# Token mixers of a hybrid decoder trunk: state products, scores and key transposes grouped over two or four token tiles

## The chip, the cores and the metric

One Trainium2 chip, one of its cores. The engines named here: PE (TensorE, matrix multiplies; PEld is its weight load), DVE (VectorE), ACT (ScalarE), POOL (GpSimd), SP (SyncE, which issues all DMAs of this kernel, in order). The metric is the device time of one execution in microseconds (us), the median of several runs; lower is better.

## The reference, cut to what matters

A two-layer decoder trunk works on a prompt of 2048 tokens of width 1024, and on eight single decode tokens. In a layer, the normalized input is multiplied by one wide projection, and its columns feed four token mixers, each a quarter of the width: A, RetNet retention; H, HGRN2; S, an S5 state space; M, Mamba-2 SSD. Their gated outputs are joined, projected by `w_out` and added to the residual. A, H and M are the same chunked recurrence, with four heads of 64 in each:

```
o_inter = einsum('bchk,bhkv->bchv', qc * exp(cum), h)          # queries against the carried state
scores  = einsum('bthk,bshk->bhts', qc, kc) * decay             # inside the chunk, causal
h_new   = exp(total) * h + einsum('bshk,bshv->bhkv', k_end, vc) # state product
o       = o_inter + einsum('bhts,bshv->bthv', scores, vc)
```

The state `h` goes from chunk to chunk. Head norm, gate and the projection follow.

## The kernel before, in words

The prompt is cut into four blocks of 512 tokens (TB), in each of two layers: eight blocks. A block is four token tiles of 128 (`tt` from 0 to 3). A Python program writes out all instructions; a list scheduler then orders each engine's instructions when the program is built, by the order in which they were written (with some offsets) and by when their inputs and buffers are expected, and adds all waits. At run time every engine works off its own list in that order.

`ORDER` is the order of writing for one block: `A`, `H`, `M`, `S` are its projections, `a`, `h`, `s`, `m` its mixers, `O` the output projection, `n`/`N` the norm for the next block, and a `^` means the block before. So a mixer is written next to projections that do not depend on it, and the scheduler places their matmuls (L647 in `gemm_wide`, L590 and L622 in `gemm`) between the mixer's steps. Weights come by DMA into raw slabs (`wr`, NWR = 7 buffers), ACT rounds them (L606, L642) and DVE makes the rest (L607, L643) into `wh` (NWH = 6 buffers); three matmuls in fp32r make one product. The first block of each layer also carries the decode tokens, for which PE multiplies with the raw slab itself (L595, L652).

PSUM has eight banks: five (`gb`) for projections, three (`mb`, `mbank()`) for all else, mixers included. Work tiles come from pools: `half` (10 buffers of 512 values per partition), `big` (9 of 1024).

Matmuls of the mixers are in float32, which the trace records as two passes for each matmul (transposes as one). `halves()` gives r = 0, 1: partitions 0 to 63 and 64 to 127. A matmul whose operands have only 64 rows (scores, L1093), or whose result has only 64 partitions (outputs L1108, L1227, L1462; state products L1113, L1233, L1468), uses half of the array.

`mix_A`, for each of the four tiles: four transposes into one bank (L1085), a copy to `qf` (L1087), scores into two banks, one for each r (L1093), multiplied by the decay mask (L1096), queries against the state `hA` (L1102), scores against values (L1108), the state product into its own bank `sp` (L1113), four DVE updates of the state into the other of two buffers (L1119). After each second tile `head_post` norms and gates the output bank `ob`, and at the end `mix_store` transposes the result (L663). `mix_H` first builds its scores in seven levels (L1183 to L1206); then, for each tile, queries against the state (L1221), scores against values (L1227), the state product (L1233) and the update (L1240), with key transposes for two tiles at a time (L1215). `mix_M`, for each tile: transposes (L1437, L1438), a decay matrix by POOL, PE and ACT (L1445 to L1449), scores (L1451) and their mask (L1453), outputs (L1462), queries against the state (L1465), the state product (L1468), the update (L1471, L1472) and the gated output.

Of the kernel before, what the change touches and what calls it, by code (L numbers as in the profile page):

```python
# [44 lines left out]
NWR = 7  # L45
# [7 lines left out]
NHN = 8  # L53
NACT = 2
# [62 lines left out]
def trunk_kernel(ctx: ExitStack, tc: tile.TileContext, A: dict):  # L117
# [959 lines left out]
    def mix_A(L, B):  # L1077
        nonlocal hA
        ogs = []
        ob = None  # L1080
        for tt in range(4):
            qk = lambda i: B.qk(tt, i)
            ps = mbank()
            for i in range(4):
                T.transpose(ps[:, i * P : (i + 1) * P], qk(i), ident)  # L1085
            qf = half()
            S.copy(qf, ps)  # L1087
            sm = half()
            smv = sm.rearrange("p (a r t) -> p a r t", a=2, r=2)
# [8 lines left out]
            if tt % 2 == 0:  # L1098
                ob = mbank()
            for p in range(2):  # L1100
                oc = (tt % 2) * 256 + p * P
                T.matmul(ob[:, oc : oc + P], qf[:, p * P : (p + 1) * P], hA[:, p, :], start=(tt % 2 == 0 and p == 0), stop=False)  # L1102
            for p in range(2):
                oc = (tt % 2) * 256 + p * P
                for r in range(2):
                    h = 2 * p + r
                    for u in range(2):
                        T.matmul(ob[64 * u : 64 * u + 64, oc + r * 64 : oc + (r + 1) * 64], sm[:, h * P + 64 * u : h * P + 64 * u + 64],  # L1108
                                 B.rv[:, tt, h * 64 : (h + 1) * 64], start=False, stop=(tt % 2 == 1 and h == 3))
            sp = mbank()  # L1110
            for p in range(2):
                for r, sl in halves():
                    T.matmul(sp[sl, p * 64 : (p + 1) * 64], qk(2 + p)[:, sl], B.rv[:, tt, p * P + 64 * r : p * P + 64 * r + 64],  # L1113
                             start=True, stop=True)
            zi[2] += 1
            hn_ = hAs[zi[2] % 2]
            for p in range(2):
                for r, sl in halves():
                    V.scalar_tensor_tensor(hn_[sl, p, sl], hA[sl, p, sl], mats[sl, M_GS + p : M_GS + p + 1],  # L1119
                                           sp[sl, p * 64 : (p + 1) * 64], ALU.mult, ALU.add)  # L1120
            hA = hn_
            if tt % 2 == 1:
                og = half([P, 4, 2, 64])
                head_post(ob.rearrange("p (t a v) -> p t a v", t=4, a=2),
                          B.rg[:, tt - 1 : tt + 1, :].rearrange("p x (b a v) -> p (x b) a v", b=2, a=2), og)
                ogs.append(og.rearrange("p t a v -> p (t a v)"))
        mix_store(B.mix, 0, lambda tt: ogs[tt // 2][:, (tt % 2) * 256 : (tt % 2) * 256 + 256], L.ret_w)
# [25 lines left out]
    def mix_H(L, B):  # L1153
# [54 lines left out]
        ogs = []  # L1208
        for tt in range(4):
            t2 = tt % 2  # L1210
            if t2 == 0:
                kps = mbank()
                for j in range(2):
                    for p in range(2):
                        T.transpose(kps[:, j * 256 + p * P : j * 256 + (p + 1) * P], k[:, p, (tt + j) * P : (tt + j + 1) * P], ident)  # L1215
                kT = half()
                S.copy(kT, kps)
                ob = mbank()
            for p in range(2):
                oc = t2 * 256 + p * P  # L1220
                T.matmul(ob[:, oc : oc + P], q[:, p, tt * P : (tt + 1) * P], hH[:, p, :], start=(t2 == 0 and p == 0), stop=False)  # L1221
            for p in range(2):
                oc = t2 * 256 + p * P
                for r in range(2):
                    h = 2 * p + r
                    for u in range(2):
                        T.matmul(ob[64 * u : 64 * u + 64, oc + r * 64 : oc + (r + 1) * 64], st[p][:, tt * 2 + r, 64 * u : 64 * u + 64],  # L1227
                                 B.gi[:, tt, h * 64 : (h + 1) * 64], start=False, stop=(t2 == 1 and h == 3))
            sp = mbank()
            for p in range(2):  # L1230
                for r, sl in halves():
                    c = p * P + 64 * r
                    T.matmul(sp[sl, p * 64 : (p + 1) * 64], kT[:, t2 * 256 + c : t2 * 256 + c + 64], B.gi[:, tt, c : c + 64],  # L1233
                             start=True, stop=True)
            zi[1] += 1
            hn_ = hHs[zi[1] % 2]
            for p in range(2):
                for r, sl in halves():
                    c = slice(64 * r, 64 * r + 64)
                    V.scalar_tensor_tensor(hn_[sl, p, c], hH[sl, p, c], tot[sl, p, tt : tt + 1],  # L1240
                                           sp[sl, p * 64 : (p + 1) * 64], ALU.mult, ALU.add)
            hH = hn_
            if t2 == 1:
                og = half([P, 4, 2, 64])
                head_post(ob.rearrange("p (t a v) -> p t a v", t=4, a=2),
                          B.gg[:, tt - 1 : tt + 1, :].rearrange("p x (b a v) -> p (x b) a v", b=2, a=2), og)
                ogs.append(og.rearrange("p t a v -> p (t a v)"))
# [160 lines left out]
    def mix_M(L, B):  # L1408
# [23 lines left out]
        ogs = []  # L1432
        for tt in range(4):
            tsl = slice(tt * P, (tt + 1) * P)
            tps = mbank()
            for j in range(2):
                T.transpose(tps[:, j * P : (j + 1) * P], xm[:, j, tsl], ident)  # L1437
            T.transpose(tps[:, 256:384], Bm[:, tsl], ident)  # L1438
            xb = half([P, 384])
            S.copy(xb, tps[:, 0:384])  # L1440
            xmT = xb[:, 0:256].rearrange("p (h v) -> p h v", h=4)
# [8 lines left out]
            cb = mbank()  # L1450
            T.matmul(cb[:, 0:256], Bm[:, tsl], cz[:, :, tsl], start=True, stop=True)  # L1451
# [3 lines left out]
            V.tensor_tensor(lv, lv, cbm[:, :, None, :].to_broadcast([P, 2, 2, P]), ALU.mult)  # L1455
            vv = half([P, 2, 4, 64])
            V.tensor_tensor(vv[:, 0], xmT, dt[:, tt, :][:, :, None].to_broadcast([P, 4, 64]), ALU.mult)
            V.tensor_tensor(vv[:, 1], vv[:, 0], ec[:, 1, tt, :][:, :, None].to_broadcast([P, 4, 64]), ALU.mult)
            ob = mbank()
            for h in range(4):  # L1460
                for u in range(2):
                    T.matmul(ob[64 * u : 64 * u + 64, h * 64 : (h + 1) * 64], lm[:, h * P + 64 * u : h * P + 64 * u + 64],  # L1462
                             vv[:, 0, h, :], start=True, stop=True)
            for g in range(2):
                T.matmul(ob[:, 256 + g * P : 256 + (g + 1) * P], cz[:, g, tsl], hM.rearrange("p a v -> p (a v)"), start=True, stop=True)  # L1465
            sp = mbank()
            for g in range(2):
                T.matmul(sp[64 * g : 64 * g + 64, 0:P], xb[:, 256 + 64 * g : 256 + 64 * g + 64],  # L1468
                         vv[:, 1, 2 * g : 2 * g + 2, :].rearrange("p a v -> p (a v)"), start=True, stop=True)
            hn_ = small([P, 2, 64], "hM")  # L1470
            V.tensor_tensor(hn_, hM, et[:, tt, :][:, :, None].to_broadcast([P, 2, 64]), ALU.mult)  # L1471
            V.tensor_tensor(hn_, hn_, sp[:, 0:P].rearrange("p (a v) -> p a v", a=2), ALU.add)  # L1472
            hM = hn_
# [18 lines left out]
            ogs.append(og)  # L1492
        mix_store(B.mix, 6, lambda tt: ogs[tt], L.m2_w)
# [145 lines left out]
    def phase(ph, i):  # L1639
# [6 lines left out]
        elif ph == "a":  # L1646
            if first:
                hA = zeroed(hAs[zi[2] % 2])
# [10 lines left out]
        elif ph == "h":  # L1659
            if first:  # L1660
                zi[1] += 1
                hH = zeroed(hHs[zi[1] % 2])
# [26 lines left out]
        elif ph == "m":  # L1689
            if first:  # L1690
                hM = zeroed(small([P, 2, 64], "hM"))
# [85 lines left out]
```

## Time and profile before

| | us |
|---|---|
| median of three runs | 2353.92 |
| runs, from lowest to highest | 2349.15 to 2357.65 |
| span of the profiled execution, from its first to its last instruction | 2351.3 |
| its PE busy | 2186.8 (93%) |
| its DVE busy | 1690.8 (72%) |
| its ACT busy | 1007.4 (43%) |

The profiled execution's own time is given as its span alone; the median is of separate executions. "Busy" of PE is the union of its modelled matmul times; a matmul's record is longer than the distance to the next one, since they are pipelined, so the pace is read from start times. A line such as L1093 is that of the kernel's file; L663 and the other lines of helpers collect the work of several callers. In the timeline each row is a run of like instructions: its start, its length, the engine, the line and the tiles, how many; in brackets the idle time before it and what ended that.

### The profile page before, as it was taken

To read this page: it belongs to the slowest core of one execution; us is meant where nothing else is said; L and a number is where in the kernel's file an instruction comes from. 1 tells how busy PE (TensorE), PEld (TensorE's weight loads), DVE (VectorE), ACT (ScalarE), POOL (GpSimd) and SP (SyncE) were. 2 spreads that over 40 slices of the span, in tenths; PEclk is the share of its full clock that TensorE was granted. 3 is DMA by queue.
4 is the path that set the end of the run, shared out by engine and by line. 5 is a ranking of instruction groups with operands and counts; after the bars stand their busy time and mean duration, and the time that the engine had idled before them with its cause. 6 is when DMAs were issued, how large, how long until landed. Compare 5 with 4: busy or idle time off the path is not lost.

```text
span 2351.3 us, 41033 instructions
## 1 busy us (share of the span) xinstructions
PE 2186.8 (93%) x15047; PEld 1724.8 (73%) x15047; DVE 1690.8 (72%) x4625; ACT 1007.4 (43%) x1873; POOL 247.0 (11%) x212
## 2 busy tenths in 40 slices
PE   7997899999989999999899987999999999999897
PEld 6766676686767877788676775776877787777687
DVE  6778885578866687558856588855985568766686
ACT  5334545245442353424534245443454344443543
POOL 1020011001111011001110001100011001100100
PEclk9998899999999999999999998999999999999998
DMA  5334543433434644251333424526244352337222
GB/s 190 89 95 103 159 154 76 129 107 118 133 101 147 139 126 141 75 167 47 125 126 114 134 65 153 162 46 182 86 153 157 104 175 64 95 122 260 64 65 83
DMA packets 259226, 283.89 MB, mean 121 GB/s; under 512 B 88208, under 2 KB 184608, under 8 KB 259024
## 3 DMA queue, kind: packets, MB, share of 16 engines
q1 hardware_dynamic: 259024, 281.26, 39.8%
q8 instruction: 119, 1.95, 0.3%
q14 instruction: 83, 0.68, 0.1%
HBM read 245.00 MB, written 31.99 MB: 118 GB/s over the span
## 4 chain that ended last, share of the span: by engine, by line
PE 57%; DVE 20%; issue 6%; ACT 3%; DMA 2%; SPq 1%; POOL 1%; ACTq 0%; DVEq 0%; POOLq 0%
PE gb L647 25%; PE gb L622 10%; PE gb L590 5%; DVE big L1191 2%; PE mb L1332 1%; PE mb L1183 1%; DVE wh L643 1%; PE mb L569 1%; DMA big<-s5c 1%; DVE hHb L1240 1%; DVE half L1299 1%; PE gb L652 1%; PE mb L663 1%; SPq L940 1%; PE mb L1198 1%
## 5 line engine op out<-in xcount | busy, mean ns | idle before, releaser
L647 PE MATMUL gb<-wh,hn 128*128 128x512 f32 x2208 | 558.0, 402 | 4.9 <-DVE wh L643 4.3
L622 PE MATMUL gb<-hn,wh 128*128 128x512 f32 x1920 | 491.5, 403 | 0.1
L647 PEld LDWEIGHTS gb<-wh,hn 128*128 128x128 f32 x2208 | 408.1, 190 | 110.3 <-issue 13.5
L622 PEld LDWEIGHTS gb<-hn,wh 128*128 128x128 f32 x1920 | 348.9, 188 | 89.4 <-issue 8.8
L642 ACT CAST wh<-wr 128x512 fp32r<-128x512 f32 x296 | 182.7, 620 | 375.9 <-PE gb L647 184.5
L647 PE MATMUL gb<-wh,mx 128*128 128x512 f32 x1344 | 338.0, 402 | 0.0
L643 DVE TENSOR_TENSOR wh<-wr,wh 128x512 fp32r<-128x512 f32 x296 | 208.6, 712 | 170.5 <-ACT wh L642 169.6
L607 DVE TENSOR_TENSOR wh<-wr,wh 128x512 fp32r<-128x512 f32 (+1 forms) x248 | 176.9, 724 | 169.5 <-ACT wh L606 163.6
L647 PEld LDWEIGHTS gb<-wh,mx 128*128 128x128 f32 x1344 | 247.7, 189 | 63.5 <-issue 6.9
L606 ACT CAST wh<-wr 128x512 fp32r<-128x512 f32 (+1 forms) x248 | 151.6, 621 | 268.1 <-PE gb L647 103.8
L590 PE MATMUL gb<-wh,hn 128*128 128x256 f32 (+1 forms) x1728 | 233.3, 291 | 4.2 <-DVE hn L553 4.1
L590 PEld LDWEIGHTS gb<-wh,hn 128*128 128x128 f32 x1728 | 218.2, 194 | 13.3 <-DVE hn L553 5.9
L1445 POOL TENSOR_TENSOR half<-mats,m_lal 128x512 fp32r<-128x512 f32 x64 | 71.7, 1148 | 511.1 <-DVE m_lal L1423 301.6
L1183 PE MATMUL mb<-zb,big 128*64 128x64 f32 x1536 | 66.5, 242 | 38.8 <-ACT zb L1176 31.5
L1191 DVE COPY_PREDICATED big<-lvl,mb 64x256 f32<-64x256 int32 x192 | 93.0, 537 | 10.3 <-PE mb L1183 6.4
L1176 ACT COPY zb<-big 64x512 f32<-64x512 f32 x112 | 70.3, 628 | 64.0 <-DVE big L1204 54.2
L1183 PEld LDWEIGHTS mb<-zb,big 128*64 128x64 f32 x1536 | 56.6, 152 | 53.5 <-ACT zb L1176 38.2
L1166 POOL TENSOR_TENSOR big<-mats,h_dg 128x1024 f32<-128x1024 f32 x16 | 34.0, 2140 | 557.8 <-DVE h_dg L1163 438.5
L1367 DVE SCALAR_TENSOR_TENSOR big<-gb,vt,big 128x511 f32<-128x511 f32 (+2 forms) x96 | 66.9, 739 | 12.0 <-ACT big L1365 11.8
L671 ACT ACTIVATE half<-mb 128x512 f32<-128x512 f32 x32 | 19.1, 598 | 88.3 <-PE mb L1227 47.8
L1348 DVE TENSOR_TENSOR half<-half,big 128x512 f32<-128x512 f32 x16 | 10.9, 687 | 63.1 <-ACT half L1347 63.1
L1042 POOL TENSOR_TENSOR half<-half,half 128x256 f32<-128x256 f32 x32 | 27.2, 850 | 235.0 <-DVE half L1040 85.2
(493 smaller groups left out, 3240.7 us busy)
## 6 DMA issues: line engine op xcount, KB each, us to landing
wr<-in_w_in SPq DMA_DIRECT2D x416, 256.0 KB
wr<-in_w_out SPq DMA_DIRECT2D x128, 256.0 KB
big<-s5c SPq DMA_DIRECT2D x56, 512.0 KB
xn<-xmid SPq DMA_DIRECT2D x32, 512.0 KB
xn<-in_x_prompt SPq DMA_DIRECT2D x24, 512.0 KB
xmid<-half SPq DMA_DIRECT2D x44, 256.0 KB
half<-xmid SPq DMA_DIRECT2D x44, 256.0 KB
half<-in_x_prompt SPq DMA_DIRECT2D x32, 256.0 KB
```

What stands on the lines that cost most here:

```text
L590: T.matmul(out, lhs[2 * ks[ki] + k][:, a, tt * P : (tt + 1) * P], hls[ki][:, c, k, :n], start=(ki == 0 and k == 0 and pi == 0 and tt % per ...
L606: S.copy(hl[:, 0, :, :n], raw[:, :, :n])
L607: V.tensor_tensor(hl[:, 1, :, :n], raw[:, :, :n], hl[:, 0, :, :n].bitcast(F32), ALU.subtract)
L622: T.matmul(banks[i], hl[:, a, k, i * P : (i + 1) * P], lhs[2 * k2 + k][:, c, :], start=(ki == 0 and k == 0 and pi == 0), stop=(ki == 3 and ...
L642: S.copy(hl[:, 0, 0:512], raw[:, 0:512])
L643: V.tensor_tensor(hl[:, 1, 0:512], raw[:, 0:512], hl[:, 0, 0:512].bitcast(F32), ALU.subtract)
L647: T.matmul(banks[tt], lhs[kt][:, a, tt * P : (tt + 1) * P], hl[:, c, 0:512], start=(kt == 0 and pi == 0), stop=(kt == KT - 1 and pi == 2))
L1176: S.copy(qz[sl, r, :].rearrange("p (b h) -> p b h", h=h), q[sl].rearrange("p a (b two h) -> p (a b) two h", two=2, h=h)[:, :, 1, :])
L1183: T.matmul(ps[su, j * 64 : (j + 1) * 64], k[:, j // 4, (j % 4) * P + 64 * u : (j % 4) * P + 64 * u + 64], qz[:, :, j * 64 + 32 * u : j * 6 ...
L1191: V.copy_predicated(stv[p][su, :, nu * u : nu * u + nu, :], mv, ps[su, p * 256 : p * 256 + 256].rearrange("p (c b h) -> p c b h", c=8, h=h))
L1367: V.scalar_tensor_tensor(acc[:, 3 - i :], ps[:, : TB - 3 + i], w(i), acc[:, 3 - i :], ALU.mult, ALU.add)
L1445: E('m').tensor_tensor(mm.rearrange("p (h t) -> p h t", h=4), tri[:, None, :].to_broadcast([P, 4, P]), lal[:, i, tt, :][:, :, None].to_bro ...
```

## The change

Scores, state products and transposes are the same matmuls in another order. `mix_A` transposes all four tiles first, makes all state products in one bank, and for each pair of tiles makes the scores of r = 0 and then of r = 1 in two banks, one mask multiply for each r, and the outputs. `mix_H` makes key transposes and state products of all four tiles first, then updates, and the outputs by pairs. `mix_M` transposes two tiles at a time, makes their state products in one bank ahead of the outputs, and the scores and the mask for both at once. States get three buffers in place of two, and raw weight slabs five in place of seven.

```diff
-NWR = 7
+NWR = 5
+NHA = 3
-    hAs = [ctile([P, 2, P], f"hAb{i}") for i in range(2)]
+    hAs = [ctile([P, 2, P], f"hAb{i}") for i in range(NHA)]
-    hHs = [ctile([P, 2, P], f"hHb{i}") for i in range(2)]
+    hHs = [ctile([P, 2, P], f"hHb{i}") for i in range(NHA)]
...
     def mix_A(L, B):
...
         for tt in range(4):
-            qk = lambda i: B.qk(tt, i)
             ps = mbank()
             for i in range(4):
-                T.transpose(ps[:, i * P : (i + 1) * P], qk(i), ident)
+                T.transpose(ps[:, i * P : (i + 1) * P], B.qk(tt, i), ident)
             qf = half()
             S.copy(qf, ps)
-            sm = half()
-            scs = [mbank(), mbank()]
+            qfs.append(qf)
+        sp = mbank()
+        for tt in range(4):
             for p in range(2):
                 for r, sl in halves():
-                    T.matmul(scs[r][:, p * P : (p + 1) * P], qf[sl, 256 + p * P : 256 + (p + 1) * P],
-                             qf[sl, p * P : (p + 1) * P], start=True, stop=True)
-            for r in range(2):
-                V.tensor_tensor(smv[:, :, r, :], scs[r][:, 0:256].rearrange("p (a t) -> p a t", a=2),
-                                gM[:, :, r, :], ALU.mult)
...
+                    T.matmul(sp[sl, tt * P + p * 64 : tt * P + (p + 1) * 64], B.qk(tt, 2 + p)[:, sl],
+                             B.rv[:, tt, p * P + 64 * r : p * P + 64 * r + 64], start=True, stop=True)
+        hs = [hA]
+        for tt in range(4):
+            zi[2] += 1
+            hn_ = hAs[zi[2] % NHA]
             for p in range(2):
                 for r, sl in halves():
...
+                    V.scalar_tensor_tensor(hn_[sl, p, sl], hs[tt][sl, p, sl], mats[sl, M_GS + p : M_GS + p + 1],
+                                           sp[sl, tt * P + p * 64 : tt * P + (p + 1) * 64], ALU.mult, ALU.add)
+            hs.append(hn_)
+            if tt % 2 == 0:
+                continue
+            scs = [mbank(), mbank()]
+            for r, sl in halves():
+                for j in range(2):
+                    for p in range(2):
+                        qf = qfs[tt - 1 + j]
+                        T.matmul(scs[r][:, j * 256 + p * P : j * 256 + (p + 1) * P], qf[sl, 256 + p * P : 256 + (p + 1) * P],
+                                 qf[sl, p * P : (p + 1) * P], start=True, stop=True)
+            sm = big()
+            smv = sm.rearrange("p (j a r t) -> p j a r t", j=2, a=2, r=2)
+            for r in range(2):
+                V.tensor_tensor(smv[:, :, :, r, :], scs[r].rearrange("p (j a t) -> p j a t", j=2, a=2),
+                                gM[:, None, :, r, :].to_broadcast([P, 2, 2, P]), ALU.mult)
+            ob = mbank()
...
     def mix_H(L, B):
...
+        sp = mbank()
+        for j in range(2):
+            kps = mbank()
+            for t2 in range(2):
+                for p in range(2):
+                    T.transpose(kps[:, t2 * 256 + p * P : t2 * 256 + (p + 1) * P], k[:, p, (2 * j + t2) * P : (2 * j + t2 + 1) * P], ident)
+            kT = half()
+            S.copy(kT, kps)
+            for t2 in range(2):
+                tt = 2 * j + t2
+                for p in range(2):
+                    for r, sl in halves():
+                        c = p * P + 64 * r
+                        T.matmul(sp[sl, tt * P + p * 64 : tt * P + (p + 1) * 64], kT[:, t2 * 256 + c : t2 * 256 + c + 64], B.gi[:, tt, c : c + 64],
+                                 start=True, stop=True)
+        hs = [hH]
         for tt in range(4):
...
     def mix_M(L, B):
...
+        xbs, vvs, hs = {}, {}, [hM]
         for tt in range(4):
+            for t in (tt, tt + 1) if tt % 2 == 0 else ():
+                tps = mbank()
...
+                vvs[t] = vv = half([P, 2, 4, 64])
...
+            if tt % 2 == 0:
+                sp = mbank()
+                for t in (tt, tt + 1):
+                    for g in range(2):
+                        T.matmul(sp[64 * g : 64 * g + 64, (t % 2) * P : (t % 2 + 1) * P], xbs[t][:, 256 + 64 * g : 256 + 64 * g + 64],
+                                 vvs[t][:, 1, 2 * g : 2 * g + 2, :].rearrange("p a v -> p (a v)"), start=True, stop=True)
+            hn_ = small([P, 2, 64], "hM", bufs=3)
...
-            cbm = half([P, 2, P])
-            V.tensor_tensor(cbm, cb[:, 0:256].rearrange("p (g t) -> p g t", g=2), tri[:, None, :].to_broadcast([P, 2, P]), ALU.mult)
+            if tt % 2 == 0:
+                cb = mbank()
+                for j in range(2):
+                    t2 = slice((tt + j) * P, (tt + j + 1) * P)
+                    T.matmul(cb[:, j * 256 : (j + 1) * 256], Bm[:, t2], cz[:, :, t2], start=True, stop=True)
+                cbm = half([P, 4, P])
+                V.tensor_tensor(cbm, cb.rearrange("p (g t) -> p g t", g=4), tri[:, None, :].to_broadcast([P, 4, P]), ALU.mult)
```

The outputs of a pair (in `mix_A` and `mix_H`) are then the matmuls of before for two tiles on end: the queries against the two states, and after them all scores against values.

## Rows read from the trace of the kernel before

**Rows 1.** The page's first part: busy us, share of the span, instructions.

```profile
span 2351.3 us, 41033 instructions
...
PE 2186.8 (93%) x15047; PEld 1724.8 (73%) x15047; DVE 1690.8 (72%) x4625; ACT 1007.4 (43%) x1873; POOL 247.0 (11%) x212
```

**Rows 2.** Waits of PE: engine and line, releaser, total us, times, longest.

```profile
PE mb L1183 <- ACT zb L1176: 31.5, 16, 5.4
...
PE mb L1462 <- DVE half L1455: 4.4, 7, 1.0
PE mb L1221 <- DVE hHb L1240: 4.3, 4, 1.6
PE gb L647 <- DVE wh L643: 4.3, 2, 3.3
```

**Rows 3.** Windows over the ends of three mixers: length, busy us (instructions) by engine.

```profile
980.00:997.00 17.00, 16.86 (x185) 13.06 (x183) 10.91 (x37) 4.80 (x10) 0.00 (x0) 1.00 0.14 47
1103.00:1116.00 13.00, 12.80 (x141) 9.48 (x139) 10.72 (x46) 4.44 (x8) 0.56 (x2) 1.00 0.20 42
1139.00:1166.00 27.00, 25.41 (x174) 17.11 (x174) 22.02 (x58) 11.19 (x25) 5.37 (x5) 1.00 0.37 116
```

**Rows 4.** Timeline of PE, one retention tile, and a pure projection.

```profile
980.48 1.18 PE L647 MATMUL gb<-wh,mx 128*128 128x512 f32 x4
981.59 0.72 PE L1093 MATMUL mb<-half 64*128 64x128 f32 x8
982.23 0.71 PE L1102 MATMUL mb<-hAb,half 128*128 128x128 f32 x4
...
983.42 0.57 PE L1108 MATMUL mb<-big,half 128*64 128x64 f32 x12
...
1004.17 33.59 PE L647 MATMUL gb<-wh,mx 128*128 128x512 f32 x144
```

**Rows 5.** Timeline of PE, the first outputs of an HGRN2 block.

```profile
1103.79 0.68 PE L1227 MATMUL mb<-big,big 128*64 128x64 f32 x14
1104.40 0.55 PE L1215 MATMUL mb<-mats,big 128*128 128x128 f32 x3
1104.88 0.33 PE L1227 MATMUL mb<-big,big 128*64 128x64 f32 x2
```

**Rows 6.** Timeline of PE, one Mamba-2 tile.

```profile
582.59 0.71 PE L1465 MATMUL mb<-hM,zb 128*128 128x128 f32 x4
583.24 0.44 PE L1468 MATMUL mb<-half,half 128*64 128x128 f32 x4
583.61 0.44 PE L1437 MATMUL mb<-mats,big 128*128 128x128 f32 x2
```

**Rows 7.** Timeline of PE, passes that all write one half.

```profile
1099.93 1.09 PE L1198 MATMUL mb<-zb,big 128*64 128x128 f32 x8
```

**Rows 8.** Timeline of PE, decoder's state product: 32 passes of one half, then 32.

```profile
390.56 0.20 PE L962 MATMUL mb<-ct,half 64*8 64x16 f32 x2
390.61 0.17 PE L961 MATMUL mb<-ct,half 64*8 64x16 f32 x1
...
390.70 0.17 PE L961 MATMUL mb<-ct,half 64*8 64x16 f32 x1
390.73 0.20 PE L962 MATMUL mb<-ct,half 64*8 64x16 f32 x2
```

**Rows 9.** Groups of instructions by line and shape, DVE: busy us, mean ns.

```profile
L1096 DVE TENSOR_TENSOR half<-mb,mats 128x256 f32<-128x256 f32 x64 | 24.8, 418 | 10.7 <-PE mb L1093 8.8 <-PE mb L1102 1.6
...
L676 DVE TENSOR_TENSOR half<-mb,big 128x512 f32<-128x512 f32 x32 | 22.1, 690 | 0.9
...
L1453 DVE TENSOR_TENSOR half<-mb,mats 128x256 f32<-128x256 f32 x32 | 13.5, 420 | 6.8 <-PE mb L1451 6.7
...
L238 DVE TENSOR_TENSOR rs<-hp_rs 128x8 f32<-128x8 f32 x96 | 17.8, 186 | 1.9
```

**Rows 10.** Waits of ACT.

```profile
ACT wh L642 <- PE gb L647: 184.5, 88, 8.2
```

More of the change, by code (lines that the diff above doesn't have):

```diff
@@ L1098, in mix_A @@
[L1098 to L1109, printed above, removed]
@@ new lines, in mix_A @@
+            smv = sm.rearrange("p (j a r t) -> p j a r t", j=2, a=2, r=2)
[5 more added lines that the diff above has]
+                for p in range(2):
+                    oc = j * 256 + p * P
+                    T.matmul(ob[:, oc : oc + P], qfs[tt - 1 + j][:, p * P : (p + 1) * P], hs[tt - 1 + j][:, p, :],
+                             start=(j == 0 and p == 0), stop=False)
@@ new lines, in mix_A @@
+            for j in range(2):
+                for p in range(2):
+                    oc = j * 256 + p * P
+                    for r in range(2):
+                        h = 2 * p + r
+                        c = j * 512 + h * P
+                        for u in range(2):
+                            T.matmul(ob[64 * u : 64 * u + 64, oc + r * 64 : oc + (r + 1) * 64], sm[:, c + 64 * u : c + 64 * u + 64],
+                                     B.rv[:, tt - 1 + j, h * 64 : (h + 1) * 64], start=False, stop=(j == 1 and h == 3))
@@ L1127, in mix_A @@
+            og = half([P, 4, 2, 64])
+            head_post(ob.rearrange("p (t a v) -> p t a v", t=4, a=2),
+                      B.rg[:, tt - 1 : tt + 1, :].rearrange("p x (b a v) -> p (x b) a v", b=2, a=2), og)
+            B.ogA.append(og.rearrange("p t a v -> p (t a v)"))
+        hA = hs[4]
+        ogs = B.ogA
         mix_store(B.mix, 0, lambda tt: ogs[tt // 2][:, (tt % 2) * 256 : (tt % 2) * 256 + 256], L.ret_w)
@@ L1208, in mix_H @@
         ogs = []
+        sp = mbank()
+        for j in range(2):
+            kps = mbank()
+            for t2 in range(2):
+                for p in range(2):
+                    T.transpose(kps[:, t2 * 256 + p * P : t2 * 256 + (p + 1) * P], k[:, p, (2 * j + t2) * P : (2 * j + t2 + 1) * P], ident)
[3 more added lines that the diff above has]
+                tt = 2 * j + t2
+                for p in range(2):
+                    for r, sl in halves():
[3 more added lines that the diff above has]
+        hs = [hH]
         for tt in range(4):
             t2 = tt % 2
[L1211 to L1234, printed above, removed]
             zi[1] += 1
-            hn_ = hHs[zi[1] % 2]
+            hn_ = hHs[zi[1] % NHA]
             for p in range(2):
@@ L1462, in mix_M @@
                     T.matmul(ob[64 * u : 64 * u + 64, h * 64 : (h + 1) * 64], lm[:, h * P + 64 * u : h * P + 64 * u + 64],
-                             vv[:, 0, h, :], start=True, stop=True)
+                             vvs[tt][:, 0, h, :], start=True, stop=True)
             for g in range(2):
[L1465 to L1473, printed above, removed]
+                T.matmul(ob[:, 256 + g * P : 256 + (g + 1) * P], cz[:, g, tsl], hs[tt].rearrange("p a v -> p (a v)"), start=True, stop=True)
             if tt % 2 == 0:
@@ L1492, in mix_M @@
             ogs.append(og)
+        hM = hs[4]
         mix_store(B.mix, 6, lambda tt: ogs[tt], L.m2_w)
@@ L1647, in phase @@
             if first:
[L1648 removed]
+                hA = zeroed(hAs[zi[2] % NHA])
             mix_A(L, B)
@@ L1690, in phase @@
             if first:
-                hM = zeroed(small([P, 2, 64], "hM"))
+                hM = zeroed(small([P, 2, 64], "hM", bufs=3))
             mix_M(L, B)
```

80 lines of the change are left out of this document (40 added, 40 removed).

## The prediction

> **What bounds the kernel now.** I read the page's first part first. TensorE (PE) is busy 2186.8 us of a span of 2351.3 us [rows 1]. So only some 165 us of the span see PE idle, and the list of PE's waits says what ends them: the largest single one is a copy inside the HGRN2 levels that the change leaves alone (31.5 us), and of those inside the changed code the two largest are 4.4 us and 4.3 us [rows 2]. Next come the windows over one retention mixer, the end of one HGRN2 mixer and one Mamba-2 mixer: PE is busy 16.86 of 17.00, 12.80 of 13.00 and 25.41 of 27.00 us [rows 3]. The reader is to see that a mixer does not stand on a path of its own: the timeline shows matmuls of the neighbouring projection (L647, L622) between its steps [rows 4], so its latency is covered, and what it costs is the PE time that it takes. The question for each edit is then how many nanoseconds of PE it adds or removes. VectorE's (DVE's) and ScalarE's (ACT's) time counts only where PE waits for it.
>
> PE's busy time hides one thing that the timeline's start times show. A pure projection runs 144 matmuls in 33.59 us, 0.233 us each. A mixer's float32 matmul is recorded as two passes. Four full-array passes of 128 columns are 0.11 us apart; eight score passes (64 rows, two halves of the array alternating) take 0.72 us, as long as four full ones (0.71) [rows 4]: two run at a time. Where all passes go to one half, eight take 1.09 us [rows 7]. And whenever PE goes from full-array passes to half-array ones and back, starts are missing. Two places give the price of such a half-array group. In the Mamba-2 mixer, from the first L1465 to the first L1437 it is 1.02 us [rows 6]; the work in it is four full passes and two double steps, 6 x 0.11 = 0.66; 0.36 is left, of which one step (0.11) belongs to the return from the group before: 0.25 us. In the retention mixer, L647 to L1093 is 1.11 us for four matmuls (0.93), and L1093 to L1102 is 0.64 us for four double steps (0.44) [rows 4]: 0.18 + 0.20 = 0.38, less some 0.08 that the return from the transposes before it had left: 0.30 us. I take 0.28 us per group.
>
> **The change part by part.** The count of matmuls, transposes, PSUM-to-SBUF copies and DMAs is the same. What differs is grouping.
>
> *Fewer half-array groups.* Before, each retention tile has two (scores; outputs with state products [rows 4]): 8 per block. After, there is one for all state products and, per tile pair, one for scores and one for outputs: 5. HGRN2 has 7 groups in the block whose first, torn one stands in [rows 5] (outputs of four tiles, one of them torn in two by the transposes, and two for state products); after, two of state products and two of outputs: 4. Mamba-2 has two per tile (L1462, L1468): 8; after, four of outputs and two of state products: 6. That is 3 + 3 + 2 = 8 groups less per block, 64 over 8 blocks: 64 x 0.28 = 17.9 us less. Bounds: 64 x 0.25 = 16.0 and 64 x 0.38 = 24.3.
>
> *Scores lose their alternation.* The old loop alternates r (the array half) innermost; the new one does all four matmuls (eight passes) of r = 0 for two tiles and then all of r = 1. Nothing in the changed mixers runs in that order now, but the decoder's state product does: 32 passes on one half, then 32 on the other. There the passes start 25 ns apart, and only around the border do both halves run: from 390.61 to 390.73 us eight start where 25 ns apart would be five [rows 8], an overlap of three passes. So a pair of tiles takes 16 - 3 = 13 steps of 0.11 us in place of 8: 5 x 0.107 = 0.53 us more, for 16 pairs 8.6 us. Bounds: no overlap at all, 16 x 8 x 0.107 = 13.7 us; full overlap, 0. I take 8.6, as the decoder's row has the same two-halves order.
>
> The Trainium skill, "TensorE: Matmul & The Clock Gate", section "The mechanism" in Part 3, says that matmuls of different array tiles overlap but start and end strictly in program order. By that rule the second half's first pass would wait for the first half's last one and the bound without overlap, 13.7 us, would hold; the decoder's rows disagree by three passes.
>
> *State updates leave the output loop.* HGRN2's output matmuls wait 4.3 us for the state updates (L1221 for hHb [rows 2]). After, the state products precede all outputs, and the first two updates can be done while the transposed keys of the second pair are made; with three state buffers the third update still waits until the first pair's outputs have read theirs. I take 3 us less, between 0 and 4.3.
>
> *Wider DVE multiplies.* Masking scores: 64 x 418 ns become 32 of 512 columns, at the 690 ns that such a multiply from PSUM takes elsewhere [rows 9]: 26.8 to 22.1 us. The Mamba-2 mask: 32 x 420 ns become 16 x 690: 13.4 to 11.0. These 7 us of DVE are hidden by projection matmuls on PE; without that cover they would give at most 7 us. In the other direction a multiply takes 0.27 us longer before the first output can start; the same cover hides it. I take 0.
>
> *State products ahead, PSUM bank held.* In the retention mixer the bank `sp` is now held from the state products to the fourth state update; with three mixer banks, two for scores are then just left, and outputs wait until the mask multiply has freed one (0.69 us). That wait is filled by projection matmuls as now. I take 0 and price it as a rival. The pair's masked scores move to the `big` pool, and four transposed tiles live at once in `half`; evictions of the previous block's output projection share `half`. Also 0, in the same rival.
>
> *Five raw weight buffers for seven.* ACT's rounding of weights waits 184.5 us for PE to free the rounded buffers [rows 10]: the weights run ahead, limited by PE and by six rounded slabs (12 matmuls, 2.8 us each), not by raw ones. Blocks that also decode differ: there PE reads the raw slab itself, and SyncE's queue (SP), where all other loads stand behind, waits for it. Two slots less delay such a slab by about 5.6 us, against six rounded slabs of cover (16.8 us) in the best case. PE's whole waiting for L643 is 4.3 us in two waits [rows 2]; I take 2 us more, between 0 and 8 (four waits like the present two, each at most doubled).
>
> Sum: -17.9 + 8.6 - 3 + 2 = -10.3 us, against the span of 2351.3: 2341.0. That span lies 2.6 us below the median of the runs shown (2353.92), inside their 2349.15 to 2357.65. I predict **2342 us** for the median of the changed kernel. Ends of the terms: -24.3 + 0 - 4.3 - 7 = -36 (2316) and -16.0 + 13.7 + 0 + 8 = +6 (2357).
>
> **The rivals.**
> 1. *Scores cost nothing:* PE's queue reaches across eight passes and runs both halves together, as it does for alternating ones. For: the decoder's border shows that the second half does start early. Against: it starts only three passes early. 2341.0 - 8.6 = 2332 us.
> 2. *Strict order on PE:* no overlap, 13.7 in place of 8.6: 2346 us. For: the overlap seen is of very short passes (16 columns). The rule of the Trainium skill named above ("TensorE: Matmul & The Clock Gate", "The mechanism") says the same.
> 3. *The groups don't stay together.* The planner places each matmul as its inputs come, and tears groups, as it did with L1227 x14 [rows 5]. If half of the 64 are regained, 9.0 us and not 17.9: 2350 us, no change.
> 4. *PSUM becomes the bound (slower).* For the second pair the retention mixer holds `sp` and the first pair's output bank, so one of the two score banks must wait until head_post has read that output bank: a reduction, eleven small operations and a multiply of 690 ns [rows 9] on DVE, some 3.4 us by my estimate (the reduction at the multiply's 0.69, the small ones at 0.186 us as L238 [rows 9]). If PE's order puts the scores before enough projection matmuls, PE stands still. Eight blocks at 3.4 us, and 16 Mamba-2 pairs whose bank is held across a tile at half of it, give 27 + 27 = 54 us uncovered; it decides from a fifth of that on (10.3 us), and at half gives 2341 + 27 = 2368 us. Against: PE idles 0.14 us in 17 in that stage now [rows 3], with projection work to spare.
>
> **How the numbers follow.** Forecast 0.40 (2335 to 2347 us), rival 1 0.14 (2318 to 2335), rival 2 0.12 (2343 to 2350), rival 3 0.19 (2347 to 2357), rival 4 0.15 (2357 to 2380). A difference below 0.3% (7 us) is about what a measurement of this kernel can't tell from none. Faster than 2346.9 are nine tenths of the forecast's cases, all of rival 1 and half of rival 2: 0.56. Slower than 2361 is rival 4 but for its lowest end, and a little of rival 3: 0.16. The rest, 0.28, is no change. The range 2320 to 2361 leaves out the best end (0.03) and most of rival 4 (0.13); the likeliest case's own range is 2335 to 2347.
>
> **What would show it.** In the changed profile, one state-product run of 32 passes per retention block, and score runs of 16 passes lasting some 1.6 us (eight double steps would be 1.1; no overlap 2.0). Half-array groups fall from 23 to 15 per block. PE's wait of L1221 for hHb is gone. The raw-weight waits of PE stay below 10 us. I am wrong if score passes still start in pairs, if new PE waits for PSUM banks (scores for head_post, or decays for hM) sum to over 10 us, or if PE's waits for rounded weights in the decoding blocks grow beyond 8 us.

## The result: slower by 1.4%, and the profile after

The changed kernel takes 2384.15 us (median; 2380.91 to 2387.44), the one before in the same comparison 2352.61 us: a ratio of 1.0137, 95% interval 1.0118 to 1.0157. I had predicted 2342 us. Below, sizes of differences are ratios times 2353 us, since each comparison ran its kernels beside the one before; the whole change costs 32.2 us so read, and a single ratio is good to some 2 to 6 us.

The page's first part, against [rows 1]:

```profile
span 2379.0 us, 40983 instructions
...
PE 2189.4 (92%) x15047; PEld 1734.6 (73%) x15047; DVE 1687.1 (71%) x4577; ACT 1011.7 (43%) x1873; POOL 242.9 (10%) x214
```

PE does the same 15047 instructions and is busy 2.6 us longer in a span 27.7 us longer. So most of the loss is PE standing still. The list of PE's waits, against [rows 2] (total us, times, longest):

```profile
PE mb L1195 <- ACT zb L1188: 28.6, 16, 6.8
...
PE mb L664 <- DVE half L678: 13.1, 9, 4.2
...
PE mb L664 <- DVE half L1518: 7.8, 7, 2.4
PE mb L664 <- DVE rs L240: 7.1, 5, 2.1
...
PE mb L1470 <- DVE half L1464: 5.6, 7, 2.8
...
PE gb L653 <- DMA wr<-in_w_out: 4.1, 2, 2.2
...
PE mb L1131 <- DVE big L1116: 2.9, 4, 1.8
PE gb L591 <- ACT wh L607: 2.7, 2, 1.8
...
PE gb L653 <- DMA wr<-in_w_in: 1.2, 1, 1.2
```

The reader is to see three things. The wait of HGRN2's outputs for their state (4.3 us in [rows 2]) has left the list, as forecast. L664, the transposes in mix_store behind each mixer, now waits 28.0 us for what ends a mixer (the last multiply of `head_post`, L678, Mamba-2's scaling L1518, the reciprocal root L240); before, the same line (L663 there) had two entries, 14.9 us in all, which [rows 2] leave out:

```profile
PE mb L663 <- DVE half L1491: 7.5, 7, 2.4
PE mb L663 <- DVE half L677: 7.4, 14, 2.1
```

And the decoder's matmuls that read raw weights (L653) wait for the weights' DMA, which they did not before.

One retention mixer on PE's timeline, against [rows 4] (start us, us, engine, line, count):

```profile
994.57 1.15 PE L1093 MATMUL mb<-big,half 128*64 128x64 f32 x32
995.65 1.71 PE L1111 MATMUL mb<-half 64*128 64x128 f32 x16
997.29 1.42 PE L648 MATMUL gb<-wh,mx 128*128 128x512 f32 x5
998.54 1.05 PE L1122 MATMUL mb<-hAb,half 128*128 128x128 f32 x8
999.53 1.15 PE L1131 MATMUL mb<-big,big 128*64 128x64 f32 x32
...
1003.05 1.05 PE L1122 MATMUL mb<-hAb,half 128*128 128x128 f32 x8
1004.76 0.34 PE L1131 MATMUL mb<-big,big 128*64 128x64 f32 x4 [0.66 <-DVE big L1116]
1005.02 0.98 PE L648 MATMUL gb<-wh,mx 128*128 128x512 f32 x3
1005.93 1.04 PE L1131 MATMUL mb<-big,big 128*64 128x64 f32 x28
```

The state products are one run of 32 passes. The scores' 16 passes take 1.64 us from L1111 to the next line's start. The second pair's outputs are torn: four passes, then projection work, then 28, with a wait for the mask multiply in front. And one pair of Mamba-2 tiles, against [rows 6]:

```profile
590.09 0.44 PE L1470 MATMUL mb<-half,half 128*64 128x128 f32 x4
590.46 0.74 PE L648 MATMUL gb<-wh,hn 128*128 128x512 f32 x2
591.03 0.40 PE L1481 MATMUL mb<-half,strict_r 128*128 128x512 f32 x1
...
592.02 0.44 PE L1470 MATMUL mb<-half,half 128*64 128x128 f32 x4
```

The state products of two tiles share a bank, but not a run: the second tile's come 1.93 us after the first's, when its DVE multiplies (L1464) are done. Counted over the whole trace, L1470 has 32 runs (16 were meant), L1131 24 (16 meant), HGRN2's outputs 16 and its state products 16 (as meant).

### The profile page after: what moved, and what is told of

It is laid out like the page before. It is cut to its first block, busy times and chain, and to the rows that moved or that the text cites. A ratio compares the mean times of both kernels' runs of the same rounds, so it can differ in the third digit from the quotient of the medians.

```text
span 2379.0 us, 40983 instructions
## 1 busy us (share of the span) xinstructions
PE 2189.4 (92%) x15047; PEld 1734.6 (73%) x15047; DVE 1687.1 (71%) x4577; ACT 1011.7 (43%) x1873; POOL 242.9 (10%) x214
## 4 chain that ended last, share of the span: by engine, by line
PE 59%; DVE 21%; issue 4%; DMA 3%; ACT 3%; POOL 1%; SPq 0%; ACTq 0%; DVEq 0%; POOLq 0%
PE gb L648 26%; PE gb L623 10%; PE gb L591 6%; DVE big L1203 2%; DMA big<-s5c 2%; PE mb L1195 2%; PE mb L1352 2%; DVE hHb L1244 1%; PE mb L1365 1%; DVE wh L644 1%; PE mb L570 1%; PE gb L653 1%; PE mb L664 1%; PE mb L1500 1%; DVE half L1319 1%
## 5 line engine op out<-in xcount | busy, mean ns | idle before, releaser
L648 PE MATMUL gb<-wh,hn 128*128 128x512 f32 x2208 | 564.2, 403 | 10.1 <-DVE half L1041 4.4
L591 PE MATMUL gb<-wh,hn 128*128 128x256 f32 (+1 forms) x1728 | 235.6, 292 | 9.9 <-DVE hn L554 5.1
L591 PEld LDWEIGHTS gb<-wh,hn 128*128 128x128 f32 x1728 | 219.1, 195 | 20.2 <-DVE hn L554 6.8
L1479 POOL TENSOR_TENSOR half<-mats,m_lal 128x512 fp32r<-128x512 f32 x64 | 71.8, 1138 | 525.9 <-DVE m_lal L1443 192.0
L1203 DVE COPY_PREDICATED big<-lvl,mb 64x256 f32<-64x256 int32 x192 | 92.9, 536 | 10.6 <-PE mb L1195 6.9
L664 PE MATMUL mb<-mats,half 128*128 128x128 f32 x192 | 32.7, 293 | 28.2 <-DVE half L678 13.1
```

The lines of the kernel that those rows point to most:

```text
L591: T.matmul(out, lhs[2 * ks[ki] + k][:, a, tt * P : (tt + 1) * P], hls[ki][:, c, k, :n], start=(ki == 0 and k == 0 and pi == 0 and tt % per ...
L648: T.matmul(banks[tt], lhs[kt][:, a, tt * P : (tt + 1) * P], hl[:, c, 0:512], start=(kt == 0 and pi == 0), stop=(kt == KT - 1 and pi == 2))
L1203: V.copy_predicated(stv[p][su, :, nu * u : nu * u + nu, :], mv, ps[su, p * 256 : p * 256 + 256].rearrange("p (c b h) -> p c b h", c=8, h=h))
L1479: E('m').tensor_tensor(mm.rearrange("p (h t) -> p h t", h=4), tri[:, None, :].to_broadcast([P, 4, P]), lal[:, i, tt, :][:, :, None].to_bro ...
```

## The experiments

All are named by what they have of the change: A is the retention mixer, H HGRN2's, M Mamba-2's; "raw" counts raw weight buffers (7 before, 5 after).

| run | mixers changed | raw | us | ratio to before, 95% interval | minus before, us |
|---|---|---|---|---|---|
| e2 | A | 7 | 2354.09 | 1.0003, 0.9990 to 1.0016 | +0.7 |
| e3 | H | 7 | 2348.65 | 0.9977, 0.9967 to 0.9986 | -5.4 |
| e4 | M | 7 | 2359.15 | 1.0016, 1.0005 to 1.0027 | +3.8 |
| e5 | A, H | 7 | 2349.49 | 0.9986, 0.9972 to 1.0001 | -3.3 |
| e12 | H | 8 | 2351.49 | 0.9989, 0.9978 to 1.0000 | -2.6 |
| e9 | none | 6 | 2355.30 | 1.0017, 1.0004 to 1.0030 | +4.0 |
| e16 | A, H | 6 | 2353.92 | 1.0003, 0.9992 to 1.0014 | +0.7 |
| e15 | M | 6 | 2366.08 | 1.0059, 1.0040 to 1.0078 | +13.9 |
| e7 | A, H, M | 6 | 2366.32 | 1.0061, 1.0038 to 1.0084 | +14.4 |
| e1 | none | 5 | 2370.78 | 1.0067, 1.0049 to 1.0084 | +15.8 |
| e6 | A, H | 5 | 2372.03 | 1.0087, 1.0068 to 1.0106 | +20.5 |
| e11 | M | 5 | 2377.83 | 1.0105, 1.0087 to 1.0124 | +24.7 |
| after | A, H, M | 5 | 2384.15 | 1.0137, 1.0118 to 1.0157 | +32.2 |

No run has all three at seven buffers.

**The parts one at a time: e1 to e4.**

```diff
e1, against before:
-NWR = 7
+NWR = 5
e2, e3, e4, against before: the hunk of the change for one function
-mix_A / mix_H / mix_M as before
+mix_A / mix_H / mix_M as changed, with its three state buffers; NWR = 7
```

> The kernel before with five raw weight buffers in place of seven, nothing else. Theory R (the raw buffers cost the time: in the changed kernel the projections' start is 6 us late after 50 us already, and falls back further only in the two blocks that decode): 12 to 20 us slower than before, with the first projections some 6 us late and both decoding blocks stretched. Theory G (the regrouped mixers themselves cost it, the buffers are hidden as the prediction had it): 0 to 4 us slower. The prediction's term was 2 us, bounds 0 and 8.

> The kernel before with the new retention mixer alone (three state buffers for it, seven raw weight buffers). Prediction's terms: 24 groups less at 0.28 us against 8.6 us of scores in order of halves: +2 us. Theory G: scores and waits for the pair's outputs make it 10 us slower or more. Theory R: within 4 us of before.

> The kernel before with the new HGRN2 mixer alone (three state buffers for it, seven raw weight buffers). Prediction's terms: 24 groups less, 6.7 us, and 3 us of waits: 10 us faster. Theory G: the transposes at the mixer's end wait longer and eat it: between 3 us faster and 6 us slower. Theory R: 6 to 10 us faster.

> The kernel before with the new Mamba-2 mixer alone (three state buffers for it, seven raw weight buffers). Prediction's terms: 16 groups less, 4.5 us faster. Theory G: the bank held across a tile and the state products ahead of the outputs add waits (5.6 us for the state products in the changed kernel): 2 to 8 us slower. Theory R: 2 to 5 us faster.

The buffers alone cost 15.8 us, half of the whole and eight times my term. The mixers alone lie between -5.4 and +3.8. Their sum with the buffers is +14.9, so some 17 us come only with the parts together.

**Pairs, and the sixth buffer: e5 to e7, e9.**

```diff
e5, e6: mix_A and mix_H as changed, mix_M as before; NWR = 7, 5
e7, against after:
-NWR = 5
+NWR = 6
e9, against before:
-NWR = 7
+NWR = 6
```

> The kernel before with the new retention and the new HGRN2 mixer (three state buffers each), the old Mamba-2 mixer and seven raw weight buffers. Theory 'sum of parts' (each part costs what it costs alone): +0.7 - 5.4 = -5 us, 2349 us. Theory 'the mixers disturb each other' (the about 17 us of the whole change that the four parts alone don't give come from the regrouped mixers together): well above that, 2354 to 2362 us. Theory 'raw buffers multiply' (those 17 us come only when five raw buffers and regrouped mixers meet): 2349 us, as the sum.

> The same as e5 with five raw weight buffers. Sum of parts: 16.5 us above e5. Raw buffers multiply: 20 to 30 us above e5. If Mamba-2's mixer is what the rest hangs on, this one lies 13 us or more below the changed kernel (at or below 2371 us); if not, within 8 us of it.

> The changed kernel with six raw weight buffers in place of five. Theory 'raw buffers are the larger part': each slot is worth some 8 us or more, 2368 to 2376 us. The prediction's step (two slots less cost 2 us): within 2 us of 2384. If raw buffers and mixers multiply, more than 10 us come back with the first slot.

> The kernel before with six raw weight buffers in place of seven, nothing else. The changed kernel with six took 2366.3 us, 18 us less than with five. If the raw buffers' cost is spread evenly over the two slots, 2361 to 2363 us; if it lies in the second slot (seven to six is free, six to five costs), 2353 to 2356 us; if in the first, 2367 to 2371 us. What the changed kernel at six has above this one is the regrouping's own.

Seven to six costs 4.0 us, six to five 11.8: the second slot carries it. Two lines' waits in e9 and e1 show where (line views of L590 and L652, the lines that are L591 and L653 after the change: idle us until the releaser, times). e9, six buffers:

```profile
  ACT wh L606: 0.2, 1
...
  DMA wr<-in_w_in: 0.3, 1
```

e1, five:

```profile
  ACT wh L606: 2.5, 2
  DVE wh L607: 1.8, 2
...
  DMA wr<-in_w_out: 4.4, 2
  DMA wr<-in_w_in: 1.3, 2
```

PE's waits for weights at these two lines, rounded and raw, go from 0.5 to 10.0 us. They fall on a projection line and on the decoder's line that reads raw slabs. The place shows in the start times too: matched one by one with the profile of before, e1's L647 matmuls start 10.6 us late at 451 us, 10.7 at 1187, 17.0 at 1317 and 13.3 at 2214. The delay grows where L652 runs, early in each layer, and not in between. A and H together are worth -3.3 us at seven buffers (e5) and at six (e16 less e9), and +4.7 at five (e6 less e1), each good to some 3 to 6 us.

**The order of the scores, and what PE's time is worth: e8 and e10.**

```diff
e8, against e5:
-            for r, sl in halves():
-                for j in range(2):
-                    for p in range(2):
+            for j in range(2):
+                for p in range(2):
+                    for r, sl in halves():
e10, against before:
-                for r, sl in halves():
+                for r, sl in [*halves(), *halves()]:
```

> e5 with the retention scores issued as before (the array half innermost, so that the two halves alternate), everything else as in e5. The prediction's term for the order of the scores: 8.6 us less than e5. Rival, that PE's saved time is not worth its length because the passes fill time in which PE would wait: 0 to 3 us less.

> The kernel before with each retention score matmul issued twice (the second overwrites the first), so that PE gets 256 more passes of that kind in the same places: about 20 us of PE time (the present scores take 21.5 us). Theory of the prediction, that a mixer costs the PE time that it takes: 2353 + 18 to 22 = 2371 to 2375 us. Rival, that part of the mixers' PE time lies in stretches in which PE would else wait for another engine: half of it or less, 2355 to 2364 us.

Timeline of e8:

```profile
988.64 1.16 PE L1112 MATMUL mb<-half 64*128 64x128 f32 x16
989.74 1.42 PE L649 MATMUL gb<-wh,mx 128*128 128x512 f32 x5
...
993.57 1.49 PE L1112 MATMUL mb<-half 64*128 64x128 f32 x16
994.98 0.96 PE L649 MATMUL gb<-wh,mx 128*128 128x512 f32 x3
...
997.75 0.34 PE L1132 MATMUL mb<-big,big 128*64 128x64 f32 x4 [0.92 <-DVE big L1117]
```

With the halves alternating, the first pair's 16 passes take 1.10 us and not 1.64; that difference of 0.54 us, for 16 pairs, would be my 8.6 us. But the second pair's run, right behind outputs, still takes 1.41 us. Over all 16 runs, from a run's first start to the next line's, e5 takes 27.05 us and e8 21.30: 5.8 us are taken out. Yet e8 takes 2352.84 us, a ratio of 0.9992 (0.9977 to 1.0007): it is not faster than e5, and the two intervals leave room for some 3.5 us at most. The last row shows what takes part of the saved time: the outputs wait 0.92 us for the mask multiply, where e5 shows 0.64 us at this place. In the lists of PE's waits, e5 and then e8:

```profile
PE mb L1132 <- DVE big L1117: 3.0, 7, 0.7
```

```profile
PE mb L1132 <- DVE big L1117: 6.5, 15, 0.9
```

Adding PE time is another matter. In e10 (timeline):

```profile
997.49 1.16 PE L1093 MATMUL mb<-half 64*128 64x128 f32 x16
998.58 0.71 PE L1102 MATMUL mb<-hAb,half 128*128 128x128 f32 x4
```

A tile's scores go from 0.64 us (981.59 to 982.23 in [rows 4]) to 1.09: 0.45 us for 32 tiles is 14.4 us. The kernel takes 2372.41 us, a ratio of 1.0082 (1.0059 to 1.0105): 19 us, between 14 and 25. This extra PE time in a mixer is paid in full; of the PE time taken out of one, most at least was not given back.

**More raw buffers: e12.**

```diff
 mix_H as changed (e3)
-NWR = 7
+NWR = 8
```

> The kernel before with the new HGRN2 mixer (e3) and eight raw weight buffers in place of seven. If a raw buffer is worth about 8 us as from seven to five: 2338 to 2342 us. If seven are enough: 2348 to 2350 us, as e3.

Seven are enough: e12 is no faster than e3.

**Mamba-2: e11, e15, e16.**

```diff
e11, e15: mix_M as changed, mix_A and mix_H as before; NWR = 5, 6
e16: mix_A and mix_H as changed, mix_M as before; NWR = 6
```

> The kernel before with the new Mamba-2 mixer and five raw weight buffers. Sum of parts: 16.5 + 3.8, 2373 to 2375 us. If the Mamba-2 mixer is what costs more with fewer raw buffers (the changed kernel lies 12 us above e6, which has the old Mamba-2 mixer): 2380 to 2386 us.

> e9 with the new Mamba-2 mixer alone. Theory 'Mamba-2 carries it': 2362 to 2367 us (7 us or more above e9, and e16 at e9's time). If the regroupings cost only together: 2357 to 2360 us (the 3.8 us that it cost at seven).

> e9 with the new retention and the new HGRN2 mixer, the old Mamba-2 mixer. At seven this pair was worth -4 us, at five +1.2. Sum of parts: 2350 to 2356 us; the step to the changed kernel at six (2366.3 us) is then Mamba-2's. If it lies above 2360 us, the pair itself suffers from the sixth buffer's loss.

At six buffers Mamba-2's regrouping alone gives the time of all three (e15 and e7), and the other two alone give the time of none (e16 and e9). On top of A and H it costs 13.7 us at six (e7 less e16) and 11.8 at five; alone 3.8 at seven, 9.9 at six, 8.9 at five.

**Is it the end of the mixers? e13 and e14.**

```diff
 in head_post and in mix_M, against e9 (e13) and e7 (e14):
-        rsqrt(rs..., ss..., 8, 1.0 / 64.0)
+        V.tensor_scalar(rs..., ss..., 0.0, 1.0, ALU.mult, ALU.add)
```

Both leave out the normalisation.

> e9 (the kernel before, six raw buffers) with the reciprocal square roots at the mixers' ends (eleven small operations on DVE in the normalisation after HGRN2 and retention, and after Mamba-2) replaced by one operation that writes 1.0; it leaves out the normalisation. PE's waits at the transposes behind the mixers were 15.6 us in e9, so some 10 us less: 2343 to 2350 us under either theory. It is the base for e14.

> e7 (the changed kernel, six raw buffers) with the same left out as in e13. Theory 'mixers' ends' (the regrouped mixers' PE work is done earlier, and PE then stands at the transposes behind them, 29.9 us in e7 against 15.6 in e9, until the normalisation on DVE is through): the distance to e13 shrinks from 11 us to 0 to 4 us. Rival, that the 11 us come from inside the regrouped mixers or from their buffers: e14 stays 8 to 14 us above e13.

e13 takes 2324.58 us (ratio 0.9880, 0.9864 to 0.9896), e14 2349.16 us (0.9979, 0.9961 to 0.9996): the distance grows from some 10 to 23 us where it should have shrunk. The theory falls. L664's waits for L678 are down to 4.5 us in e14, but no other wait took their place in the list at such a size. PE's busy time and its clock do differ between the two (page's first part and mean granted clock; e13, then e14):

```profile
span 2321.3 us, 40535 instructions
...
PE 2172.0 (94%) x15047; PEld 1716.7 (74%) x15047; DVE 1630.5 (70%) x4097; ACT 1010.3 (44%) x1875; POOL 248.2 (11%) x212
```

```profile
core 0: 2321.3 us, clock 0.978
```

```profile
span 2355.4 us, 40464 instructions
...
PE 2191.3 (93%) x15047; PEld 1739.2 (74%) x15047; DVE 1626.3 (69%) x4049; ACT 1007.6 (43%) x1873; POOL 243.7 (10%) x214
```

```profile
core 0: 2355.4 us, clock 0.967
```

The clock has two levels, and the granted share is 1 at 2.4 GHz and 0.5 at 1.2; so the time at the lower one is twice the missing share: 0.022 x 2 x 2321 = 102 us in e13, 0.033 x 2 x 2355 = 155 us in e14. Of the 53 us more, up to half is PE work lost, 27 us, and PE's busy time is 19.3 us longer for the same instructions. These two executions are 34.1 us apart in span, and e14's is the slowest of its ten. Over all executions the mean clocks are 0.9765 and 0.9694, by the same reckoning some 17 us of PE work, between medians 24.6 us apart. That the lower clock carries the distance is not shown: no run set the clock by itself, and e5, with the same 15047 instructions, has PE busy for only 2183.4 us at a clock of 0.969.

**Which part of Mamba-2's? e17 and e18.**

```diff
e17, against e7:
-            for t in (tt, tt + 1) if tt % 2 == 0 else ():
+            for t in (tt,):
...
-                for t in (tt, tt + 1):
-                    for g in range(2):
-                        T.matmul(sp[...], xbs[t]..., vvs[t]...)
 and behind each tile's outputs:
+            sp = mbank()
+            for g in range(2):
+                T.matmul(sp[...], xbs[tt]..., vvs[tt]...)
 ... and the state's update behind them
e18, against e7:
-            if tt % 2 == 0:
-                cb = mbank()
-                for j in range(2): ...
+            cb = mbank()
+            T.matmul(cb[:, 0:256], Bm[:, tsl], cz[:, :, tsl], start=True, stop=True)
 ... and the mask multiply tile by tile
```

> e7 (the changed kernel, six raw buffers, 2366.3 us) with the Mamba-2 state products, their transposes and the state update tile by tile again, behind each tile's outputs; the shared bank for the decays of two tiles stays. Theory 'state products ahead': the 12 us that the Mamba-2 regrouping costs at six (e7 against e16, 2353.9) come from the state products' being ahead of the outputs for two tiles (PE waits for the DVE multiplies that feed them, and DVE does the work of two tiles before the first output): 2353 to 2358 us. Rival 'shared bank' (the matmul and the mask multiply of two tiles): 2363 to 2368 us.

> e7 with the Mamba-2 matmuls of C and B and their mask multiply tile by tile again, and the state products of two tiles ahead as changed. Theory 'state products ahead': 2363 to 2368 us. Rival 'shared bank': 2353 to 2358 us. If both lie between, the two share it.

Both miss: e17 takes 2378.43 us (1.0103, 1.0085 to 1.0120), e18 2370.88 us (1.0069, 1.0051 to 1.0086), against e7's 2366.32. Undoing either part alone makes it slower, so neither alone is what costs; the two were not undone together. What both kept is the place of the state's two DVE multiplies, ahead of the decays and the mask multiply (before, they came behind it); that was not tried alone.

## Why the prediction was wrong

**The step that failed first: "I take 2 us more, between 0 and 8" for five raw buffers.** It measured 15.8 us (e1), and in the changed kernel the sixth slot alone gives 17.9 us back (e7). My cover was six rounded slabs, and the waits of ACT [rows 10] show that weights run ahead of PE in plain blocks. But in the blocks that also decode PE reads the raw slab itself, and a slot is held until it has; with five, PE then waits for slabs at both lines. I had named these blocks and then priced their delay by the cover of the others. I had also asked that PE's waits for raw weights stay below 10 us. They do (5.3 us at L653 in the changed kernel, 5.7 at L652 in e1), and the price is almost three times the waits. None of my three signs of being wrong came up, and the kernel is 42 us off.

**The second: "how many nanoseconds of PE it adds or removes".** The PE terms but one came out nearly as costed. A run of scores takes the 13 steps that I gave it, 1.64 us, and 1.10 where the halves alternate in full (e8's first pairs): 0.54 us against my 0.53, so rival 1 (no cost) and rival 2 (strict order, 2.0 us a run) are out at the passes' level. By the Trainium skill's rule that I weighed ("TensorE: Matmul & The Clock Gate", "The mechanism" in Part 3: tiles overlap, but start and end in program order) a run would take 16 steps; the 1.64 us of L1111 disagree. HGRN2's state wait is gone. Of the 64 half-array groups only 40 are regained (A 2 a block, H 3, M none): rival 3 is half true, and that term is 11.2 us at my price, not 17.9. By my terms A alone should have cost 8.6 - 6.7 = 1.9 us, H given 6.7 + 3 = 9.7 and M given 4.5; at seven buffers they measured +0.7, -5.4 and +3.8. What failed is what such time is worth. PE's time taken out of a mixer turned, in part at least, into waits for DVE: 5.8 us less of score time gave nothing that the runs can tell (e8), with 3.5 us more of waits for the mask multiply, and L664 now waits 28.0 us. I counted DVE's wider multiplies and the chain behind the mixers as hidden by projection matmuls, and left L663's 14.9 us of waits behind the mixers unweighed. The mixer's windows [rows 3] did show PE busy nearly throughout; they did not show how much of that was needed to cover DVE.

**What the waits cost beyond their length.** At one HGRN2 mixer's end after the change (timeline, then windows, whose last three columns are the granted clock, the DMA share and GB/s):

```profile
1126.28 1.15 PE L1261 MATMUL mb<-big,big 128*64 128x64 f32 x32
1127.36 4.18 PE L623 MATMUL gb<-hn,wh 128*128 128x512 f32 x17
1133.64 0.63 PE L664 MATMUL mb<-mats,half 128*128 128x128 f32 x4 [2.10 <-DVE rs L240]
...
1135.99 1.11 PE L664 MATMUL mb<-mats,half 128*128 128x128 f32 x4 [0.89 <-DVE half L678]
```

```profile
1127.00:1134.00 7.00, 4.90 (x37) 3.79 (x32) 6.74 (x30) 3.70 (x5) 1.23 (x2) 1.00 0.06 14
1134.20:1141.00 6.80, 5.92 (x25) 5.03 (x24) 5.63 (x12) 4.25 (x8) 2.08 (x2) 0.50 0.26 77
1141.00:1148.00 7.00, 7.00 (x42) 5.51 (x41) 5.43 (x15) 4.61 (x9) 0.00 (x0) 1.00 0.49 153
```

PE is busy 4.90 of 7.00 us, waiting 2.10, and in the next 6.80 us the clock is at 0.50, its lower level: four of L664 take 1.11 us there and 0.63 at its border. Before, the like waits at this mixer's end (L663, from 1116 us) were 0.29 and 0.16 us, and the clock was at 1.00 from 1110 to 1138 us. Over the whole kernel the clock's mean is 0.971 after and 0.973 before, 138 and 127 us at the lower level, up to 5.5 us of PE work. But that profile is the fastest of the changed kernel's four executions; the other three show 0.966, by which it would be up to 17 us. A lower clock by itself doesn't make the loss, though: e5's ten executions show 0.967 to 0.973, against 0.971 to 0.976 before, and e5 is no slower than before. The Trainium skill, "TensorE: Matmul & The Clock Gate", "HAM oscillation — how this bites in real kernels", tells of matmul groups that each start at half clock behind a wait; these rows agree in that the lower clock follows a wait, here of 2.10 us. How the changed kernel's 32 us split between this and the waits is not settled.

**Rival 4 (PSUM) didn't happen:** L1111 waits 0.2 us in all, and the only like wait in the list is 1.7 us of the outputs (L1122) for head_post (L677). The slower outcome came by another way than the one that I gave it.

**The account.** Along one path of runs: raw buffers 15.8 us (e1), A and H with five buffers +4.7 (e6), M on top +11.8 (after): 32.2. Shown are the first, with its place, and that M's part is not in the other mixers. Some 4 us of M's part stand in every trace with its new mixer, at the end of the last block, where the last output projection surrounds the last Mamba-2 mixer. The views of its 384 matmuls, with first and last start (L590 in e9; the same line is L592 in e15), and then a row of e15's timeline (L1452 and L1446 there are L1470 and L1464 of the changed kernel):

```profile
L590 PE MATMUL gb<-wh,mx x384: 275/281/419, 2280.0 to 2346.6; 128*128 128x256 f32 x192
```

```profile
L592 PE MATMUL gb<-wh,mx x384: 275/281/775, 2278.4 to 2349.1; 128*128 128x256 f32 x192
```

```profile
2291.54 0.44 PE L1452 MATMUL mb<-half,half 128*64 128x128 f32 x4 [2.81 <-DVE half L1446]
```

From first start to last it takes 66.6 us in e9 and 70.7 in e15; at seven buffers 66.6 and 70.8 (e4), at five 66.5 (e1) and 70.8 (e11), and with A and H at five 67.7 (e6) and 72.0 (the changed kernel). The state products, now ahead, wait there 2.81 us for DVE's multiply. Placing them behind the outputs again didn't cure it (73.8 us in e17). Open stays the rest of M's 12 us: the profiles of e9 and e15 are 2.6 us apart in span (2358.0 and 2360.6), their medians 10.8, so the trace of one execution doesn't hold it.

Of all versions e3 (HGRN2's mixer alone, seven buffers) is the fastest with the whole computation: 0.9977, within what I called no change.

## What to carry to other kernels

Price a buffer that is taken away in the stage that uses it directly, not in the one that has another buffer behind it; a run with the count alone costs one line and would have shown half of this loss. PE time in a mixer was paid in full when added (e10) and, as far as the runs can tell, not given back when removed (e8): before regrouping matmuls, ask what DVE must have done by then. And grouping in the source is no grouping on the engine where the second half of the inputs comes later: Mamba-2's state products stayed as many runs as before.

## What the runs showed that I had not expected

The second of two buffers cost three times the first (4.0, then 11.8 us), and an eighth gained nothing. Twelve small DVE operations replaced by one in each of 48 normalisations (4625 - 4097 = 528 fewer) are worth 32 us together (e13 against e9: 0.0137 of 2353 us), with 63.8 us less of DVE's busy time (1694.3 to 1630.5). PE's waits at L663 fall from 15.0 us to 1.8: the chain at a mixer's end is where this kernel has time to give, whether by its latency or by DVE's load was not tried apart. And PE's busy time for the same 15047 instructions varies by 19 us (2172.0 to 2191.3 us) between e13 and e14.
